# Seven block products for the last four gate tiles of a fused transformer layer

## The chip, the cores and the metric

The kernel runs on one core of a Trainium2 chip. The metric is the device time of one execution in microseconds (us). A core has five engines with queues of their own: TensorE (PE in the profile; its weight loads are PEld), VectorE (DVE), ScalarE (ACT), GpSimd (POOL) and SyncE (SP), which here only issues DMAs. They meet through semaphores. Operands lie in SBUF, matmul results in eight PSUM banks of 128x512 float32.

## The reference, cut to what matters

One layer, 1024 tokens, width 1024. The input is modulated, projected by one large matrix, and the last 2048 columns of that projection, after a sigmoid, gate the two attention branches:

```python
h = x * (1.0 + scale1) + shift1
proj = h @ w_in + b_in                       # q, k, v of both branches, then the gates
g_a, g_b = jnp.split(jax.nn.sigmoid(proj[..., OFF_GA:]), 2, axis=-1)
y = (g_a * (o_a @ w_branch_a) + g_b * (o_b @ w_branch_b)) @ w_out
```

The attention, the LayerNorms and a convolutional feed-forward part follow. The 2048 gate columns are 16 tiles of 128 columns. A gate tile is a 128x1024 block of the transposed weight times the 1024x1024 input `h`.

## The kernel before, in words

Each float32 factor is split into a high part rounded to the matmul type and the low rest (`split`, L335 to L342: a cast, then a subtraction). A product is three matmuls, high by high, high by low, low by high (`mm3`, L344 to L347), each 128x128 by 128x512.

The projection stage is a list `steps`, walked in one loop (L966). First come the q columns of branch B, then by `GORD` (L39) three gate tiles, the first half of q of branch A (group "qa"), four gate tiles, its second half ("qb": the change's title calls it the second q half), four gate tiles (7 to 10), group "ka" (keys and values of token tiles 0 to 4), gate tile 11, group "kb" (token tiles 5 to 7 and the two context tiles, called 8 and 9), and gate tiles 12 to 15. A gate tile is two steps, one for each half of the tokens (`gate`, L908): eight input tiles `hT[k]`, each a pair of high and low 128x1024 tiles, times the weight pieces, 24 matmuls a step. A step of kb is 15 matmuls.

Weights come by SP five steps ahead (`wload1`, three `raw` buffers) and are split three steps ahead (`wpair`, `wsplit`, four pairs of `wp` buffers): high part on ScalarE, low part on VectorE for q, k and v, on GpSimd for the gates.

Beside the steps runs a queue of side work. `side_step` (L932) takes one more entry from it and gives each entry in flight its next stage. `kv_post` (L628) is the side work of a key/value tile: stage 1 adds the bias out of PSUM and turns the first key (VectorE), copies the values (ScalarE, GpSimd) and takes the norm (its power on GpSimd, L555); stage 2 turns the second key and splits both into `ks`; stage 3 transposes `ks` on TensorE (`ktr`, L664). Two `kv` buffers serve the ten tiles, so a tile starts when the one two before it is through. `qprep` is that of the first two attention units. `mods` doles out 48 reductions (L445) that make the modulation vectors, from weights that SP loads (`mload`); the last falls into ka.

Through ka, VectorE and SP take the source order (`manual_schedule`, L959). After it all engines, and TensorE all along, take an order that a scheduler fixes when the kernel is built: it prefers what stands earlier in the source, among what it holds to be ready. On the chip each engine follows the fixed list.

Memory: 19 slots of 4 KB a partition (`ht`, `hput`). After ka all are taken: eight by the q tiles `Q0_t` and `Q1_t` of the two branches, ten by keys and values, one by the rotary table `ropet`. The attention stage follows with an order of its own for all engines; unit by unit it reads the q tiles, branch A first.

## Time and profile before

| | us |
|---|---|
| three runs | 1531.91, 1532.15, 1530.88 (median 1531.91) |
| profiled execution | 1530.37 |
| its span, first to last instruction | 1528.6 |
| TensorE busy in the span | 1512.9 |
| VectorE / ScalarE / GpSimd busy | 1144.8 / 802.1 / 773.5 |
| last gate matmul ends, attention starts | about 333.5 after the span's start |

In the rows of a timeline the columns are start, duration, engine, source line, operation, output, inputs, shapes and count; in brackets stands the idle time of the engine before the instruction and what ended it. In rows of groups they are line, engine, operation, output from inputs, shapes and count, then busy us and mean ns of one, then idle us and what ended it. A row of a stretch gives its length, then busy us and instruction count of each engine, the granted TensorE clock, the busy share of the DMA engines and GB/s. Matmuls overlap: the cost of one in a row is the distance of two starts, not the duration shown.

### The profile page before, as it was taken

The page shows a single profiled execution, that of the slowest core. Times are in us where ns is not written, and L with a number is a line of the kernel's source. Part 1 is how long each engine was busy: PE and PEld are TensorE (multiplying, and loading weights), DVE is VectorE, ACT ScalarE, POOL GpSimd, SP SyncE. Part 2 cuts the span into 40 slices and gives each one's busy share as a digit, 9 for nine tenths or more (in the row PEclk, how much of TensorE's full clock was granted, in tenths as well). Part 3 has the DMA queues.
Part 4 walks back from the last instruction along what each step waited for, and adds up shares of the span by engine and source line. Part 5 has one row for each costly group of instructions (what it writes and reads, how often), then busy time and mean ns, then how long its engine had stood idle before and what let it go on. Part 6 is the DMA issues. An engine that isn't in the chain of part 4 may idle for free. (4 is left out here: it accounts for less than half of the span.)

```text
span 1528.6 us, 21924 instructions
## 1 busy us (share of the span) xinstructions
PE 1512.9 (99%) x7652; PEld 1269.9 (83%) x7652; DVE 1144.8 (75%) x1719; ACT 802.1 (52%) x1404; POOL 773.5 (51%) x737
## 2 busy tenths in 40 slices
PE   9999999999999999999999999999999999999997
PEld 7888888888988888888788988888888888888886
DVE  7488847627776777787665878888888887656797
ACT  5422223449887777798332574444444444435543
POOL 0365303418887565574333556666676674021063
PEclk9999999999999999999999999999999999999999
DMA  9667663312256663742460222333334446996723
GB/s 379 236 234 254 213 239 110 100 49 56 57 151 157 176 149 79 169 95 68 169 173 35 97 86 108 112 110 112 112 102 111 110 111 177 373 281 207 253 91 111
DMA packets 111873, 229.73 MB, mean 150 GB/s; under 512 B 13489, under 2 KB 27313, under 8 KB 111666
## 3 DMA queue, kind: packets, MB, share of 16 engines
q1 hardware_dynamic: 96464, 199.20, 39.0%
q0 software_dynamic: 10400, 20.19, 8.4%
q10 hardware_dynamic: 4898, 8.94, 1.6%
q8 instruction: 60, 0.98, 0.3%
q14 instruction: 51, 0.42, 0.1%
HBM read 177.09 MB, written 65.87 MB: 159 GB/s over the span
## 5 line engine op out<-in xcount | busy, mean ns | idle before, releaser
L1151 DVE TENSOR_TENSOR lo<-pt,hi 128x512 fp32r<-128x512 f32 x188 | 126.4, 688 | 42.8 <-ACT hi L1145 41.3
L342 DVE TENSOR_TENSOR ld<-rd,hd 128x1024 fp32r<-128x1024 f32 x77 | 97.8, 1287 | 49.6 <-ACT hd L337 47.4
L1145 ACT CAST hi<-pt 128x512 fp32r<-128x512 f32 x188 | 109.6, 584 | 47.3 <-PE pt L808 39.1
L337 ACT CAST hd<-rd 128x1024 fp32r<-128x1024 f32 x77 | 79.4, 1050 | 85.8 <-PE p L347 55.7
L345 PE MATMUL p<-hd 128*128 128x512 f32 x264 | 103.2, 391 | 0.0
L346 PE MATMUL p<-ld,hd 128*128 128x512 f32 x264 | 102.8, 389 | 0.2 <-DVE ld L342 0.2
L347 PE MATMUL p<-hd,ld 128*128 128x512 f32 x264 | 102.8, 389 | 0.0
L817 PE MATMUL av<-lo,VT 128*128 128x512 f32 x236 | 101.5, 435 | 0.2 <-POOL lo L1151 0.2
L817 PE MATMUL av<-hi,VT 128*128 128x512 f32 x236 | 100.5, 433 | 0.0
L347 PE MATMUL g<-hh,wlg 128*128 128x512 f32 x256 | 99.7, 390 | 0.4 <-POOL wlg L342 0.4
L345 PE MATMUL g<-hh,whg 128*128 128x512 f32 x256 | 99.9, 390 | 0.0
L346 PE MATMUL g<-hl,whg 128*128 128x512 f32 x256 | 99.6, 389 | 0.0
L754 DVE TENSOR_SCALAR_CACHE_REDUCE p<-s,cvt,nmc 128x1024 f32<-128x1024 f32 x64 | 85.8, 1340 | 16.4 <-PE s L721 9.3
L342 POOL TENSOR_TENSOR wlg<-wg,whg 128x512 fp32r<-128x512 f32 x32 | 45.3, 1423 | 99.3 <-ACT whg L337 93.7
L763 ACT ACTIVATE p<-p,nm 128x1024 f32<-128x1024 f32 x64 | 74.0, 1157 | 13.0 <-DVE p L754 12.4
L808 PE MATMUL pt<-ident,p 128*128 128x128 f32 x512 | 76.8, 272 | 0.0
L808 PEld LDWEIGHTS pt<-ident,p 128*128 128x128 f32 x512 | 62.7, 140 | 15.4 <-DVE lo L1151 0.2
L337 ACT CAST wS<-s 128x512 fp32r<-128x512 f32 x76 | 45.3, 620 | 52.1 <-POOL s L1465 51.3
L720 PE MATMUL s<-KL,q 128*128 128x512 f32 (+2 forms) x184 | 72.4, 393 | 0.0
L721 PE MATMUL s<-KL,q 128*128 128x512 f32 (+2 forms) x184 | 69.0, 375 | 0.2 <-DMA q<-q 0.2
L337 ACT CAST wA<-ru 128x512 fp32r<-128x512 f32 x57 | 35.5, 623 | 59.6 <-PE d L347 31.8
L342 DVE TENSOR_TENSOR wS<-s,wS 128x512 fp32r<-128x512 f32 x57 | 55.5, 1000 | 11.1 <-ACT wS L337 11.1
(432 smaller groups left out, 5019.2 us busy)
## 6 DMA issues: line engine op xcount, KB each, us to landing
wml<-in_wmodT_dram SPq DMA_DIRECT2D x48, 512.0 KB
ru<-in_w_up_dram SPq DMA_DIRECT2D x38, 512.0 KB
rd<-td SPq DMA_DIRECT2D x55, 256.0 KB
rd<-sd SPq DMA_DIRECT2D x44, 256.0 KB
rd<-in_w_dn_dram SPq DMA_DIRECT2D x33, 256.0 KB
wm<-in_wmodT_dram SPq DMA_DIRECT2D x16, 512.0 KB
wg<-in_w_g_dram SPq DMA_DIRECT2D x32, 256.0 KB
sgd<-sg ACTq DMA_DIRECT2D x32, 256.0 KB
```

Source lines behind the costliest of these rows:

```text
L337: cast[:] = [nc.scalar.copy(hi, src).ins]
L342: low[:] = [lo_eng.tensor_tensor(out=lo, in0=src, in1=hi.bitcast(F32), op=ALU.subtract).ins]
L345: nc.tensor.matmul(ps, a[0], b[0], start=start, stop=False, skip_group_check=resumed)
L346: nc.tensor.matmul(ps, a[0], b[1], start=False, stop=False, skip_group_check=resumed)
L347: return nc.tensor.matmul(ps, a[1], b[0], start=False, stop=stop, skip_group_check=resumed).ins
L720: nc.tensor.matmul(o, self.q1[:, hs], ks, start=True, stop=False)
L754: nc.vector.tensor_scalar(out=p if self.br else p[:, self.pad + 1:SINK + 1], in0=self.sv[h], scalar1=self.scale()[:, hs] if self.br else - ...
L763: nc.scalar.activation(o, i, AF.Exp, bias=self.nm[:, hs], scale=-1.0, accum_out=acc)
L808: nc.tensor.transpose(tr[:, h * P:(h + 1) * P], src, ident)
L817: nc.tensor.matmul(self.av, v, self.parts[n][low], start=first, stop=self.left == 0)
L1145: nc.scalar.copy(hi, units[u].parts[n])
L1151: e.tensor_tensor(out=lo, in0=src, in1=hi.bitcast(F32), op=ALU.subtract)
```

## The change

Gate tile 11 moves from before kb to behind it, and tiles 12 to 15 are done otherwise. Two tiles are a pair. The pair's weights are a 2x2 matrix of blocks (tile by half of the 1024 inputs), `h` is a 2x2 matrix of blocks (half of the inputs by half of the tokens), and the eight block products of their product become seven, P1 to P7, of sums of blocks: fourteen `product` steps for two pairs, each four input tiles times three matmuls, 12 matmuls.

- **Input sums.** Sums need exact float32 inputs, so `x` is loaded again (`xload`, eight tiles of 512 KB), modulated (`xscale`, ScalarE) and summed in place (`xsums`, four subtractions of 128x512 for each pair of input tiles k and k+4, VectorE). They lie in the slots of the q tiles, which are first written to device memory (`away`, eight times 512 KB) and read back near the end (`qback`). Of the four groups of sums, group 0 and group 1 stand in gate tiles 9 and 10 (these, 7 to 10, follow the second q half), group 2 in ka, group 3 behind the first product. Summed inputs are split (`tsplit`) by ScalarE into the second halves of `hT[0..3]`, which gate tile 11 reads last, and into new tiles `TL[0..3]`: `TL[0]` takes the slot of `ropet`, `TL[k]` that of input tile k+3. The low parts of P6 are GpSimd's, the others VectorE's.
- **Weight sums.** P1, P2 and P4 use plain blocks and the old loads. The other blocks are loaded by `block_in`; `bsums` (GpSimd, four sums a pair) makes P5's, P6's, P7's and P3's weights of them. The first pair's blocks a11 and a22 go into the slot of input tile 7.
- **Outputs.** VectorE adds products out of PSUM (`vsum`, five a pair), then sigmoid and store as before.
- **Order.** From gate tile 11 to the end of the stage TensorE takes the source order.

The diff, cut to its core:

```diff
-GORD = 3, 4, 4, 1, 4
+GORD = 3, 4, 4, 0, 1
+    SRC = {"P1": (0, 0), "P2": (0, 1), "P4": (1, 1)}
+    SUM = {"P5": (0, 0), "P7": (1, 0), "P6": (1, 1), "P3": (0, 1)}
...
+    plain = len(steps)
+    steps += [("s", n, p) for n, p in (("P1", 0), ("P1", 1), ("P2", 0), ("P2", 1), ("P4", 0), ("P4", 1), ("P6", 0),
+                                       ("P5", 0), ("P6", 1), ("P5", 1), ("P7", 0), ("P7", 1), ("P3", 0), ("P3", 1))]
+    def away(br, t):
+        nc.sync.dma_start(qd[br, t], Q[br, t])
+    def xplace(k):
+        return ((1, 0), (1, 4), (0, 2), (0, 6), (1, 2), (1, 6), (0, 4), (0, 0))[k]
+    def xload(k):
+        X[k] = onto(hslot["Q%d_%d" % xplace(k)], [P, T], F32, f"xs{k}")
+        nc.sync.dma_start(X[k], xT[k])
+    def xsums(k):
+        a, b = k, k + 4
+        for o, p, q in ((xs(a, 1), xs(a, 1), xs(a, 0)), (xs(b, 1), xs(b, 1), xs(a, 1)),
+                        (xs(b, 0), xs(b, 0), xs(b, 1)), (xs(a, 0), xs(b, 1), xs(a, 0))):
+            nc.vector.tensor_tensor(out=o, in0=p, in1=q, op=ALU.subtract)
+    todo = {(7, 0): [(away, 1, 0), (away, 1, 2)], (7, 1): [(away, 1, 4), (away, 1, 6)],
+            (8, 0): [(xload, 0), (xload, 4)], (8, 1): [(xload, 1), (xload, 5)], (9, 0): [(xscale, 0)],
+            (9, 1): [(xscale, 1), (xsums, 0)], (10, 0): [(xsums, 1)], ("ka", 0): [(away, 0, 2)],
+            ("ka", 1): [(away, 0, 4)], ("ka", 2): [(xload, 2), (away, 0, 6)], ("ka", 3): [(xload, 6), (away, 0, 0)],
+            ("ka", 4): [(xload, 3)], ("ka", 5): [(xscale, 2)], ("ka", 6): [(xsums, 2)]}
+    TP = {"P4": (4, 0, 0), "P6": (4, 1, 1), "P5": (0, 1, 0), "P7": (0, 0, 1)}
+    def tsplit(n, k):
+        d, hf, m = TP[n]
+        hi = hT[k][m][:, HALF:T]
+        if k not in TL:
+            TL[k] = onto(hslot["Q%d_%d" % xplace(3 + k) if k else "ropet"], [P, T], R32, f"tl{k}")
+        split(xs(d + k, hf), hi, TL[k][:, hsl(m)], nc.scalar, nc.gpsimd if n == "P6" else nc.vector)
...
+        if n == plain - 2:
+            inorder.enter_context(tc.manual_schedule(engines={mybir.EngineType.PE}))
+        if gi == "s":
+            product(k, a)
+            m = n - plain
+            side_step()
+            if m == 0:
+                xsums(3)
+                for q in (3, 0, 1, 2):
+                    tsplit("P4", q)
+                    tsplit("P6", q)
+                block_in(0, 1, 0, bias_place("b21a"))
+                t = onto(hslot["Q0_0"], [P, 2, HALF], F32, "bA")
+                block_in(0, 0, 0, t[:, 0])
+                block_in(0, 1, 1, t[:, 1])
+            elif m == 1:
+                bsums(0, 0)
+            elif m == 3:
+                for b in ((1, 1, 0), (1, 0, 0), (1, 1, 1), (1, 0, 1), (0, 0, 1)):
+                    block_in(*b, pw("b%d%d%d" % b))
+            elif m == 4:
+                with tc.issue_after(last_sum[0]):
+                    bsums(1, 0)
+                    bsums(0, 1)
+                    bsums(1, 1)
+            elif m == 5:
+                for q in range(4):
+                    tsplit("P5", q)
+            elif m == 8:
+                qback((0, 0, 7))
+                for q in range(4):
+                    tsplit("P7", q)
+                qback((0, 2, 0), (0, 4, 1), (0, 6, 2), (1, 0, 3))
+            elif m == 11:
+                qback((1, 2, 4), (1, 4, 5), (1, 6, 6))
+            continue
         if gi == "g":
             gate(k, a)
+            early(k, a)
+            if n >= plain - 2:
+                if a == 0:
+                    xload(7)
+                else:
+                    xscale(3)
```

## The prediction

> **What bounds the kernel now.** I read the first lines of the page, then TensorE's timeline and ScalarE's sigmoids at the end of the projection stage.

> ```profile
> span 1528.6 us, 21924 instructions
> PE 1512.9 (99%) x7652; PEld 1269.9 (83%) x7652; DVE 1144.8 (75%) x1719; ACT 802.1 (52%) x1404; POOL 773.5 (51%) x737
> ```

> TensorE is busy for 99% of the span, so work taken from it counts in full unless a new wait fills the place.

> ```profile
> 247.35 0.39 PE L345 MATMUL g<-hh,whg 128*128 128x512 f32 x1
> ...
> 258.24 0.46 PE L664 MATMUL ktr<-identr,ks 128*128 128x128 f32 x4
> 258.53 0.46 PE L345 MATMUL acckb<-whkb,hh 128*128 128x512 f32 x1
> ...
> 287.83 0.39 PE L347 MATMUL acckb<-whkb,cl 128*128 128x512 f32 x1
> ```

> Gate tile 11 takes 258.24 - 247.35 = 10.89 us for 48 matmuls, 0.227 each: a row's 0.39 is not its cost. A group of four transposes costs 0.29. kb ends at 288.1.

> ```profile
> 328.24 0.69 ACT L920 ACTIVATE sg<-g,bgc 128x512 f32<-128x512 f32 x1 [4.75 <-PE g L347]
> 333.68 0.69 ACT L920 ACTIVATE sg<-g,bgc 128x512 f32<-128x512 f32 x1 [4.76 <-PE g L347]
> 334.39 1.28 ACT L1010 ACT_TABLE_LOAD   x1
> 336.40 1.23 POOL L1029 TENSOR_SCALAR pa<-negsink 128x1 f32<-128x1 f32 x8
> 336.62 0.73 ACT L763 ACTIVATE pa<-pa,nm 128x513 f32<-128x513 f32 x1 [0.73 <-POOL pa L1029]
> ```

> The last steps follow each other every 5.44 us, the time of their 24 matmuls, and ScalarE waits for TensorE each time: the end of the stage is TensorE's alone.

> **What goes.** Eight half tiles of 24 matmuls become fourteen products of 12: 192 become 168. The 24 that go are one such step: **-5.44 us**. Nothing else leaves or enters TensorE; gate tile 11 and the transposes only move.

> **What is added on the way there.** I looked at the stretches in which the q tiles leave and three groups of sums are made, and at an early one for the DMA rate.

> ```profile
> 20.00:40.00 20.00, 20.00 (x90) 16.57 (x89) 17.86 (x25) 12.39 (x12) 0.00 (x0) 1.00 1.03 405
> 177.00:200.00 23.00, 23.00 (x104) 19.03 (x103) 17.19 (x19) 5.27 (x9) 12.90 (x9) 1.00 0.61 213
> 220.00:247.40 27.40, 27.40 (x123) 22.69 (x122) 16.87 (x34) 6.18 (x10) 3.24 (x2) 1.00 0.57 183
> 207.22 0.69 DVE L342 TENSOR_TENSOR wlka<-wka,whka 128x512 fp32r<-128x512 f32 x1 [12.99 <-ACT whka L337]
> L478 ACT ACTIVATE xr<-xr,modc 128x1024 f32<-128x1024 f32 x7 | 8.7, 1245 | 0.2
> ```

> DMA: four stores and four loads of 0.52 MB in some 22 us add 190 GB/s to 213: 403, what the early stretch moved (405). In ka four stores, three loads and the kb loads that now come sooner, about 4.6 MB in 27.4 us, add 168 to 183: 351. It fits, if barely; at the lower rate that 183 GB/s at a share of 0.57 implies (321) ka's loads end 2.6 us late. SP stands in order with weight loads behind a store's wait, but each reload has two steps, 6.8 us or more, behind its store, and weights are split three steps ahead. Cost 0; without that cover up to 2.6.

> VectorE's groups 0 and 1 fall beside a wait of 12.99 us; I take each sum as a low part's subtraction, 0.6 (below). Group 2 and its scaling (two of 1.25) stand in ka, where VectorE has 10 us free and ScalarE 21; the low weights of kb queue behind them three steps early. Cost 0, or the group's 2.4 if that lead is used up.

> kb now follows ka at once, so its side work loses the cover of gate tile 11.

> ```profile
> 246.60:272.40 25.80, 25.80 (x130) 21.47 (x129) 24.87 (x97) 11.57 (x34) 11.11 (x14) 1.00 0.28 90
> 246.60 0.68 DVE L633 TENSOR_TENSOR kv<-accka,bias_kv 128x512 f32<-128x512 f32 x1
> 248.00 0.68 DVE L633 TENSOR_TENSOR kv<-accka,bias_kv 128x512 f32<-128x512 f32 x1
> ```

> kb wants five PSUM banks while ka still holds five of eight. Two are emptied by 248.7; the fourth is wanted at 247.4 + 9 x 0.227 = 249.4. Cost 0, or the 0.7 of one such add. VectorE is 24.87 of 25.80 busy while it serves ka's five tiles, packing 0.964; kb's end is 276.9 now (288.1 - 10.89 - 0.29), so this work still ends before.

> **The place that decides** is from there to P6. Its first VectorE work, tile 5 of kb, is complete at 285.54 - 11.18 = 274.4.

> ```profile
> 289.39 0.28 DVE L559 TENSOR_TENSOR kv<-kv,ssk 128x128 f32<-128x128 f32 x1
> 290.26 1.37 DVE L559 TENSOR_TENSOR kv<-kv,ssk 128x128 f32<-128x128 f32 x1
> 290.20 1.29 POOL L342 TENSOR_TENSOR wlg<-wg,whg 128x512 fp32r<-128x512 f32 x1
> 285.54 1.37 DVE L633 TENSOR_TENSOR kv<-acckb,bias_kv 128x512 f32<-128x512 f32 x2 [2.52 <-PE acckb L347]
> ```

> The same VectorE instruction takes 0.28 alone and 1.37 when GpSimd started 0.06 before it; it ends just behind GpSimd's. So most SBUF work of the two engines runs one after the other. [...]

> ```profile
> 258.50 0.68 DVE L342 TENSOR_TENSOR wlkb<-wkb,whkb 128x512 fp32r<-128x512 f32 x1
> 259.10 0.28 DVE L532 TENSOR_TENSOR ktp<-kv,ropet 128x128 f32<-128x128 f32 x1
> L559 DVE TENSOR_TENSOR kv<-kv,ssk 128x128 f32<-128x128 f32 x5 | 1.6, 322 | 0.4 <-POOL ssk L555 0.4
> L341 DVE CAST ks<-kv 128x256 fp32r<-128x256 f32 x5 | 1.4, 281 | 0.0
> L342 DVE TENSOR_TENSOR ks<-kv,ks 128x256 fp32r<-128x256 f32 x5 | 2.1, 411 | 0.0
> L540 DVE TENSOR_TENSOR kv<-ktp 128x128 f32<-128x128 f32 x6 | 1.7, 281 | 0.0
> L538 DVE TENSOR_TENSOR ktp<-kv,tbk 128x64 f32<-128x64 f32 x6 | 1.1, 212 | 0.0
> L532 DVE TENSOR_TENSOR ktp<-kv,tbk 128x128 f32<-128x128 f32 x3 | 0.8, 278 | 0.0
> L342 POOL TENSOR_TENSOR wlg<-wg,whg 128x512 fp32r<-128x512 f32 x6 | 7.8, 1296 | 4.9 <-ACT whg L337 4.9
> L645 POOL TENSOR_TENSOR VT<-kv,VT 128x256 fp32r<-128x256 f32 x5 | 3.9, 781 | 4.1 <-ACT VT L637 4.0
> L655 POOL TENSOR_TENSOR kv<-kv,gcol 128x128 f32<-128x128 f32 x2 | 0.9, 460 | 0.6 <-PE g L347 0.4 <-DVE kv L559 0.2
> ```

> VectorE, kb's five tiles: 1.6 + 1.4 + 2.1, two turns of three tiles 1.7 + 12 x 0.212 + 6 x 0.278, in all 11.0 for 39 instructions; successive ones overlap by 0.08 (0.68 against a distance of 0.60), so 7.9. With the last group of sums (4 x 0.6), P4's low parts (4 x 0.6) and P6's first low weight (0.6): 13.3. GpSimd: five weight splits 6.5 (P1 to P4 but the first), 3.9, 0.9, P6's low parts 4 x 1.3, two weight sums 2 x 1.3 (two inputs of that size, as in the split): 19.1. Together **32.4 us**.

> TensorE in source order, from 276.9: gate tile 11 10.9, five transposes 1.5, P1 and P2 10.9: the transposes of tile 9 are due at 300.2; with them and two P4 (0.3 + 5.4) P6 is due at 305.9. From 274.4 that is 31.5. Packed without a gap the sums are 0.9 late, at packing 0.964 (33.6) 2.1. Bounds: 0, if part of it overlaps, and 9.2 (below). I take the middle of the packed two, **+1.5**, since that row is the nearest.

> Behind the stalled P6 are only products. P5's and P7's splits have one product and their own first chunks (2.7 + 2) as cover for four casts and four subtractions of 0.6, which chase each other; the rest of the weight sums has 10 us of GpSimd. The 4 MB read back go while DMA is at 0.11.

> ```profile
> 307.40:333.50 26.10, 26.10 (x122) 21.64 (x121) 0.00 (x0) 4.88 (x8) 2.59 (x2) 1.00 0.11 41
> PE pt L808 <- ACT pa L763: 0.7, 2, 0.4
> ```

> VectorE's zero there is room for the ten output adds. At the hand-over the last sigmoid stands behind one more add, 0.7. Attention's first exponential waits for GpSimd at 336.62, 0.7 after the table load and its small exponential; so **+0.1**, or 0.7 at most. The two waits of TensorE (0.7) stay.

> **Sum:** -5.44 + 1.5 + 0.1 = -3.8: 1530.37 becomes 1526.5 for the profiled execution (1.8 of it outside the span). The median shown is 1.54 higher, 1531.91, so the forecast is **1528.1**. A run of this kernel can't tell less than 0.2%, 3.1 us, from no change: the bounds are 1528.8 and 1535.0.

> **The rivals.**

> *No wait at all* (0.13). The engines overlap more than I count: -5.3, **1526.6**. For it: VectorE's adds from PSUM, and GpSimd's powers (L555) beside which VectorE rows aren't long. Against: the stretch at 0.964.

> *The reload is late* (0.30). P4's and P6's splits form a ring: `TL[3]` needs the slot of input tile 6, which `q=2` reads last, and so on, while a11 and a22 need the slot of input tile 7, which `q=3` reads. If all but P6's weight is done first, 29.2 / 0.964 = 30.3, it starts at 304.7.

> ```profile
> 242.97 0.90 SPq L873 DMA_DIRECT2D cx<-in_ctxT_dram  x2
> 245.53 0.60 ACT L877 ACTIVATE cx<-cx,modx 128x256 f32<-128x256 f32 x1 [0.98 <-DMA cx<-in_ctxT_dram]
> ```

> A load takes 2.6; then two sums 2.6 and the split 1.3: ready at 311.2, 5.3 late. -5.44 + 5.3 + 0.1: **1531.9**, the same. For it: this order in the source. Against: tiles 8 and 9 can fill the load's gap.

> *Source order holds TensorE at tile 9* (0.25), the case on the other side. Before, the scheduler put these transposes where it liked; now P4 stands behind them. Tile 9's second stage stands behind the tile sums and the weight sums in the source. If VectorE and GpSimd take these first, its `ks` comes after 32.4 + 1.3 (third sum) = 33.7, 35.0 packed: 309.4 against 300.2, 9.2 late. -5.44 + 9.2 + 0.1 = +3.9: **1535.8**. It decides slower from a wait of 8.4 on, `ks` behind 308.6. [...] Against: before, tile 9 was through in 22 us.

> That the change does not do what it says would be a hand-over that isn't TensorE's; the sigmoid rows exclude more than the 0.7 above.

> **How the numbers follow.** The forecast case, a wait of 0.5 to 2.4, has 0.32; with no wait 0.13 that makes faster 0.45, same 0.30, slower 0.25. The forecast, likeliest by little and beside the no-wait case in sign, alone has 1527.1 to 1529.0. The range goes from 1526.2 (no wait, a little spread) to 1537.0 (the slower rival and the 0.7 of the hand-over).

> **What would show it.** 24 matmuls fewer; 168 under the product tiles at 0.227. In the list of waits, TensorE before P6's first matmul, for VectorE's low weight: 1 to 2 us; 5 us there speaks for the reload; a wait of the `ktr` transposes for VectorE `ks` of 9 us for the source order. The stretch from 274 to 306 with VectorE and GpSimd nearly full. What would make me wrong elsewhere: TensorE waiting in ka or kb for low weights (DMA too slow, or VectorE behind group 2), or at P7, or in the first attention units for a q tile read back late.

## The result, and the profile after

The changed kernel takes 1546.47 us (median of 4 runs, 1545.1 to 1547.27) against 1531.43 of the kernel before beside it: ratio 1.0097, 95% interval 1.008 to 1.0115. It is 15 us slower, where 3.8 us faster was forecast. The profiled execution took 1545.1 us, 1.8 of it outside the span. Each profile read below shows one execution; those of e11 and e19 are the slowest of their kernels' runs, that of e17 the fastest.

The first lines of the page, changed kernel:

```profile
span 1543.3 us, 22040 instructions
PE 1516.0 (98%) x7628; PEld 1268.2 (82%) x7628; DVE 1186.3 (77%) x1765; ACT 824.7 (53%) x1436; POOL 792.2 (51%) x747
```

TensorE has 24 instructions fewer (7628 for 7652) and is yet busy for 3.1 us more: some of its matmuls became slower. The span is 14.7 longer, so the rest of the loss is idle time. Where it lies, the stretches between TensorE's stage borders show. In each row: length, busy us and count of each engine, granted TensorE clock, DMA share, GB/s. First the kernel before, kb and then gate tiles 12 to 15:

```profile
258.53:288.06 29.53, 29.53 (x147) 24.56 (x146) 20.24 (x64) 14.18 (x44) 12.55 (x14) 1.00 0.39 119
288.06:333.48 45.42, 45.42 (x213) 37.69 (x212) 16.15 (x50) 12.60 (x32) 13.73 (x16) 1.00 0.16 57
```

The changed kernel, in order: kb; gate tile 11 and P1 of both pairs; P2 of both (behind a wait of 2.2 us, which no row shows); P4 of both with the wait before P6; P6 of the first pair; P5 of the first; the other six products:

```profile
246.47:282.06 35.59, 32.23 (x145) 25.35 (x144) 34.33 (x112) 15.88 (x44) 13.47 (x15) 0.95 0.36 111
282.06:299.91 17.85, 17.85 (x89) 14.71 (x87) 16.29 (x49) 8.01 (x22) 9.66 (x12) 1.00 0.14 46
302.12:308.40 6.28, 6.28 (x33) 5.18 (x33) 4.35 (x7) 4.91 (x15) 4.26 (x5) 1.00 0.57 173
308.40:318.21 9.81, 6.21 (x26) 4.24 (x26) 1.75 (x2) 0.62 (x1) 8.21 (x7) 0.99 0.33 107
318.21:323.90 5.69, 5.65 (x12) 4.01 (x13) 3.74 (x3) 3.32 (x7) 5.53 (x5) 0.50 0.14 49
323.90:330.58 6.68, 4.61 (x13) 2.83 (x12) 6.62 (x8) 2.29 (x6) 3.41 (x3) 0.76 0.21 78
330.58:347.74 17.16, 17.16 (x73) 13.94 (x72) 10.51 (x15) 7.59 (x12) 0.93 (x2) 0.97 0.67 222
```

kb: 35.59 against 29.53, **+6.1**, VectorE busy 34.33 of it. Between the second and third row TensorE stands still: **+2.2** before P2. The fourth row should be two products, 2 x 2.72: **+4.4**. P6: 5.69 for 2.72 at a clock of 0.50, **+3.0**. P5: **+4.0**. Six products in 17.16 for 16.32: **+0.8**. In all +20.5; less the 5.44 saved, and less 0.9 because ka ends at 246.47 and not 247.35, that is 14.2: the stage ends at 347.74 and not 333.48. The last 0.4 of the span lies behind the stage.

TensorE's waits in the changed kernel, those of 1 us or more that the kernel before has not (us in all, times, longest):

```profile
PE ktr L670 <- DVE ks L343: 2.3, 1, 2.3
PE ly L346 <- ACT whP L338: 2.2, 1, 2.2
PE lz L347 <- DVE tl L343: 2.1, 2, 1.3
PE lx L346 <- ACT u L1080: 2.0, 1, 2.0
PE lw L348 <- POOL wlgP L343: 1.4, 1, 1.4
PE sx L727 <- DMA q<-q: 1.0, 1, 1.0
```

The first five lie in this stage, in kb, P6, P5, P2 and P4, and each ends with another instruction, on three engines; no single culprit stands there. (`lx`, `lw`, `ly`, `lz` are the banks of P1 and P2, P4, P6 and P7, P5 and P3; `u` is P1's copy, `tl` the low inputs `TL`, `whP` and `wlP` the split of a summed weight, `wlgP` the low part of a plain one, `b`, `b21a` and `bA` the loaded blocks, `bA` a11 and a22; L338 is the cast of a split, L343 its subtraction, L670 the transposes, L866 `block_in`, L1051 `bsums`.) The last, 1.0 us, is a new wait in attention, at 479 us, far behind its first units. The timelines of three places tell how the waits arise.

**kb.** TensorE waits 2.25 us with a transpose, and kb's matmuls stand behind it. VectorE and GpSimd at that time:

```profile
270.39 0.29 DVE L565 TENSOR_TENSOR kv<-kv,ssk 128x128 f32<-128x128 f32 x1 [0.18 <-POOL ssk L561]
270.60 1.48 DVE L343 TENSOR_TENSOR ks<-kv,ks 128x256 fp32r<-128x256 f32 x1
```
```profile
270.45 1.35 POOL L343 TENSOR_TENSOR wlg<-wg,whg 128x512 fp32r<-128x512 f32 x1
272.14 0.37 PE L670 MATMUL ktr<-identr,ks 128*128 128x128 f32 x2 [2.25 <-DVE ks L343]
```

The `ks` subtraction, 0.41 alone, takes 1.48: GpSimd's split began 0.15 before it, and it ends 0.28 behind that split (272.08, 271.80). The prediction saw the same in the trace before (1.37 for 0.28) and counted on it one stage later. It makes 1.1 of the 2.25 us; the rest is that VectorE came to this tile late: its cast began at 269.92, when TensorE was waiting already.

**P6.** GpSimd, then SP, ScalarE and VectorE of the changed kernel:

```profile
310.45 1.75 POOL L343 TENSOR_TENSOR tl<-xs,hl 128x512 fp32r<-128x512 f32 x1
312.15 1.29 POOL L343 TENSOR_TENSOR wlgP<-wP,whgP 128x512 fp32r<-128x512 f32 x1
314.88 1.29 POOL L1051 TENSOR_TENSOR b21a<-bA,b21a 128x512 f32<-128x512 f32 x1 [1.44 <-DMA bA<-in_w_g_dram]
316.25 1.26 POOL L1051 TENSOR_TENSOR bA<-bA,b21a 128x512 f32<-128x512 f32 x1
318.82 6.44 POOL L1051 TENSOR_TENSOR b<-b,b 128x512 f32<-128x512 f32 x4
312.22 0.80 SPq L866 DMA_DIRECT2D bA<-in_w_g_dram  x2
317.54 0.62 ACT L338 CAST whP<-bA 128x512 fp32r<-128x512 f32 x1 [10.51 <-POOL bA L1051]
318.19 2.90 DVE L343 TENSOR_TENSOR wlP<-bA,whP 128x512 fp32r<-128x512 f32 x2 [7.16 <-ACT whP L338]
324.06 4.05 DVE L343 TENSOR_TENSOR tl<-xs,hh 128x512 fp32r<-128x512 f32 x3
```

That is the rival "the reload is late", step by step: the last reader of input tile 7's slot ends at 312.20, SP issues the reload at 312.22, GpSimd gets it at 314.88, two sums, ScalarE's cast at 317.54, P6 at 318.21. VectorE's low part of that weight then takes 2.90 for two and P5's low parts 4.05 for three, beside GpSimd's four sums of 1.61: 1.4 each for 0.6.

**The clock.** TensorE's timeline in kb, from the third matmul behind the wait on:

```profile
273.38 0.39 PE L348 MATMUL acckb<-whkb,hl 128*128 128x512 f32 x1
273.61 0.59 PE L346 MATMUL acckb<-whkb,hh 128*128 128x512 f32 x1
273.99 0.63 PE L347 MATMUL acckb<-wlkb,hh 128*128 128x512 f32 x1
274.42 0.63 PE L348 MATMUL acckb<-whkb,hl 128*128 128x512 f32 x1
...
276.98 0.43 PE L348 MATMUL acckb<-whkb,ch 128*128 128x512 f32 x1
277.25 0.39 PE L346 MATMUL acckb<-whkb,ch 128*128 128x512 f32 x1
```

From 273.61 to 277.0 the starts are 0.43 apart and not 0.23: half clock for 3.4 us, 1.5 us behind the end of a wait of 2.25. These matmuls take 1.6 us more than at full clock. The stretch doesn't, however: e4 below has kb with the same work at a clock of 1.00, and its kb takes 36.38 us, VectorE busy for 35.16 of them; it is VectorE that sets its length.

### The profile page after: what moved, and what is told of

Read it like the earlier page. It is cut to its first block, busy times and chain, and to the rows that moved or that the text cites. A ratio compares the mean times of both kernels' runs of the same rounds, so it can differ in the third digit from the quotient of the medians.

```text
span 1543.3 us, 22040 instructions
## 1 busy us (share of the span) xinstructions
PE 1516.0 (98%) x7628; PEld 1268.2 (82%) x7628; DVE 1186.3 (77%) x1765; ACT 824.7 (53%) x1436; POOL 792.2 (51%) x747
## 4 chain that ended last, share of the span: by engine, by line
PE 86%; DVE 6%; DMA 2%; POOL 2%; issue 2%; ACT 1%; SPq 0%; DVEq 0%; ACTq 0%; POOLq 0%
PE av L823 7%; PE pt L814 6%; PE s L726 3%; PE s L727 3%; PE g L348 3%; PE g L347 3%; PE g L346 3%; PE p L348 2%; PE p L346 2%; PE p L347 2%; PE c L346 2%; PE d L346 2%; PE a L348 2%; PE a L346 2%; PE c L348 2%; PE d L348 2%
## 5 line engine op out<-in xcount | busy, mean ns | idle before, releaser
L343 DVE TENSOR_TENSOR ld<-rd,hd 128x1024 fp32r<-128x1024 f32 x77 | 96.6, 1271 | 51.1 <-ACT hd L338 47.5
L338 ACT CAST hd<-rd 128x1024 fp32r<-128x1024 f32 x77 | 79.5, 1050 | 87.8 <-PE p L348 61.4
L347 PE MATMUL p<-ld,hd 128*128 128x512 f32 x264 | 103.2, 391 | 0.4 <-DVE ld L343 0.4
L348 PE MATMUL g<-hh,wlg 128*128 128x512 f32 x192 | 74.9, 390 | 0.4 <-POOL wlg L343 0.4
L346 PE MATMUL g<-hh,whg 128*128 128x512 f32 x192 | 75.0, 391 | 0.0
L347 PE MATMUL g<-hl,whg 128*128 128x512 f32 x192 | 74.8, 390 | 0.0
L338 ACT CAST wS<-s 128x512 fp32r<-128x512 f32 x76 | 45.2, 620 | 51.7 <-POOL s L1656 50.9
L338 ACT CAST wA<-ru 128x512 fp32r<-128x512 f32 x57 | 35.5, 623 | 61.7 <-PE d L348 33.2
L1345 POOL TENSOR_TENSOR lo<-ptr,hi 128x512 fp32r<-128x512 f32 x48 | 62.5, 1301 | 2.0
L343 DVE TENSOR_TENSOR wS<-s,wS 128x512 fp32r<-128x512 f32 x57 | 56.8, 1024 | 4.9 <-ACT wS L338 4.9
```

What stands on the lines that cost most here:

```text
L338: cast[:] = [nc.scalar.copy(hi, src).ins]
L343: low[:] = [lo_eng.tensor_tensor(out=lo, in0=src, in1=hi.bitcast(F32), op=ALU.subtract).ins]
L346: nc.tensor.matmul(ps, a[0], b[0], start=start, stop=False, skip_group_check=resumed)
L347: nc.tensor.matmul(ps, a[0], b[1], start=False, stop=False, skip_group_check=resumed)
L348: return nc.tensor.matmul(ps, a[1], b[0], start=False, stop=stop, skip_group_check=resumed).ins
L1345: e.tensor_tensor(out=lo, in0=src, in1=hi.bitcast(F32), op=ALU.subtract)
```

## The experiments

The theory after the trace: **the seven products are too close to their inputs.** The chain of splits and sums on VectorE, GpSimd and ScalarE is longer than the matmul work that covers it, each consumer in TensorE's fixed list waits in turn, and each wait may cost a stretch of half clock. The rivals: TensorE's source order; the one late reload; kb's lost neighbour; the sums in ka. The time holds more than the stage: from the stage's end to the span's end the traces of these kernels have 1194.0 us (e8) to 1198.5 (e14), though no edit is aimed there. So where a difference is of 2 us or less, the stage's end in the trace stands beside the time.

| kernel | us | ratio to before, 95% |
|---|---|---|
| e1: only gate tile 11 moved | 1532.97 | 1.0009 (0.9999 to 1.0019) |
| e2: without the source order | 1546.26 | 1.0098 (1.0083 to 1.0113) |
| e3: reload into other buffers | 1545.74 | 1.0098 (1.0081 to 1.0114) |
| e4: weight sums on VectorE | 1541.53 | 1.0065 (1.005 to 1.008) |
| e6: third group of sums later | 1543.66 | 1.0086 (1.0069 to 1.0103) |
| e7: filler before P6 | 1546.18 | 1.0097 (1.0082 to 1.0112) |
| e8: gate tile 10 behind kb too | 1537.87 | 1.0043 (1.0028 to 1.0058) |
| e9: e8 and weight sums on VectorE | 1533.85 | 1.002 (1.001 to 1.003) |
| e10: a gate tile between ka and kb | 1539.3 | 1.0055 (1.0041 to 1.0068) |
| e11: gate tiles between and behind | 1531.79 | 1.0003 (0.9994 to 1.0013) |
| e12: e11, second P6 before first P5 | 1531.89 | 1.0006 (0.9997 to 1.0015) |
| e13: e12, ka's transposes later | 1531.95 | 0.9999 (0.999 to 1.0008) |
| e14: the change, ka's transposes later | 1549.19 | 1.0109 (1.0096 to 1.0123) |
| e15: e13, kb's work first | 1535.22 | 1.0019 (1.001 to 1.0028) |
| e16: e12, kb's work first | 1535.68 | 1.0027 (1.0016 to 1.0037) |
| e17: e15, kb's transposes later too | 1533.49 | 1.0013 (1.0004 to 1.0022) |
| e18: e17, source order from P1 on | 1533.54 | 1.0012 (1.0003 to 1.0021) |
| e19: e17, P1 copied by VectorE | 1533.38 | 1.0008 (0.9999 to 1.0017) |

**e1, gate tile 11 alone** (in the kernel before):

```diff
-GORD = 3, 4, 4, 1, 4
+GORD = 3, 4, 4, 0, 5
```

> The kernel before with one thing of the change: gate tile 11 goes behind group kb instead of between ka and kb (GORD 3, 4, 4, 0, 5); no products, no early stores, loads or sums. Theory A, kb's 6.5 us of waits and slow clock in the changed kernel come from the missing gate tile (VectorE has to finish ka's five tiles and kb's splits in kb's own 29 us): kb takes 33 to 36 us here too and the time is 1534 to 1538. Theory B, they come from the third group of input sums and its loads, which this kernel lacks: kb takes under 31 us and the time stays within 1 us of 1531.4.

kb takes 30.74 us, 1.2 more than before, and the interval of the ratio reaches down to no change. Neither theory in full: the missing gate tile is about 1.2 of kb's 6.1 us.

```profile
247.68:278.42 30.74, 29.84 (x146) 24.25 (x144) 30.04 (x102) 13.91 (x41) 15.67 (x17) 1.00 0.36 108
```

VectorE is busy 30.04 of 30.74: it has no room left here for the sums.

**e6, the third group of sums later** (in the changed kernel):

```diff
-            ("ka", 4): [(xload, 3)], ("ka", 5): [(xscale, 2)], ("ka", 6): [(xsums, 2)]}
+            ("ka", 4): [(xload, 3)], ("ka", 5): [(xscale, 2)]}
...
+                xsums(2)
                 xsums(3)
```

> The changed kernel with its third group of input sums (four subtractions on VectorE) issued behind kb with the fourth, and not at ka's seventh step. Theory A, that group stands ahead of kb's own work on VectorE, which is full there (18.7 of 20 us): without it kb takes 31 to 33 us instead of 35.6, and behind kb the 2.4 us come back in part: 1542 to 1545. Theory B, kb is late for another reason (the loads, or kb's splits by themselves): kb stays above 35 us and the time rises by up to 2 us.

```profile
246.85:279.29 32.44, 29.94 (x146) 24.35 (x144) 31.59 (x109) 15.40 (x43) 13.74 (x15) 1.00 0.42 130
```

Theory A: kb loses 3.1 us less. So kb's 6.1 are 1.2 (e1), 3.1 of the sums, and some 1.7 not taken apart; with the sums in ka, kb takes 35.6 to 36.6 in five traces (the changed kernel, e2, e3, e4, e7), so these sizes are good to about 1 us. The time falls by 2.8.

**e2, without TensorE's source order**: the line that enters it at `plain - 2` is taken out.

> The changed kernel without TensorE's source order behind kb: the scheduler places its instructions from gate tile 11 on. Theory A, TensorE waits for data that come late whatever its order: the time stays at 1544 to 1548. Theory B, the source order is what makes TensorE stand idle while other products could run: the waits before P2, P4 and P6 (6 us in all) shrink and the time is 1541 or less.

The time stays, and so do the waits. Row by row TensorE's list up to the end of the stage is the same in both traces: left alone, the scheduler chooses the source order too. So forcing it cost nothing; whether another order would wait less this run can't tell.

**e3, the reload elsewhere**:

```diff
-                t = onto(hslot["Q0_0"], [P, 2, HALF], F32, "bA")
-                block_in(0, 0, 0, t[:, 0])
-                block_in(0, 1, 1, t[:, 1])
+                block_in(0, 0, 0, raw("a11"))
+                block_in(0, 1, 1, raw("a22"))
```

> The changed kernel with the blocks a11 and a22 of the first pair loaded into two buffers of the ring of raw weights, which are free once P2's and P4's weights are split (about 306 and 309 us), and no longer into the slot of input tile 7 (free at 312.2). Theory A, P6 of the first pair waits for this reload and the clock falls behind that wait: P6 starts 1.5 to 3 us earlier, its 12 matmuls take about 3 us instead of 5.7, and the time falls by 3 to 5 us, to 1541 to 1543. Theory B, GpSimd and ScalarE are the bound of that chain (the weight sums and splits of P2 to P6 in one line): P6 starts less than 1 us earlier and the time falls by less than 1.5 us.

P6 waits no more, and the time is less by 0.7 only. P4 of both pairs with what follows, P6, P5:

```profile
308.18:318.06 9.88, 7.45 (x27) 5.63 (x26) 4.27 (x4) 1.88 (x4) 9.72 (x7) 0.83 0.42 135
318.06:321.40 3.34, 2.94 (x13) 2.07 (x11) 1.50 (x2) 1.61 (x4) 3.26 (x4) 1.00 0.24 83
321.40:329.01 7.61, 5.13 (x13) 3.02 (x13) 7.61 (x8) 2.58 (x6) 4.89 (x4) 0.78 0.00 0
```

P6 starts at 318.06, as before at 318.21. GpSimd is busy 9.72 of the 9.88 us ahead of it: it did a weight sum first, P4's low weight came later (a wait of 2.4 for 1.4), and the slow clock moved to P4. The reload was what ended the last wait, but without it GpSimd's work alone lasts as long. Theory B. In this trace the stage ends at 345.67, 2.1 earlier, and the part behind it is 1.9 longer: the reload may hold up to 2 us of the loss, not the 3 to 5 of theory A.

**e4, the weight sums on VectorE**:

```diff
-            last_sum[:] = [nc.gpsimd.tensor_tensor(out=o, in0=a, in1=b, op=op).ins]
+            last_sum[:] = [nc.vector.tensor_tensor(out=o, in0=a, in1=b, op=op).ins]
```

> The changed kernel with the eight weight sums on VectorE instead of GpSimd. Theory A, VectorE's low parts for P5 (4.05 us for one row in the profile) are blocked by GpSimd's sums beside them, 1.6 us each: with the sums on VectorE at 0.6 us each P5's two products lose under 2 us instead of 4 and P6's weight is ready about 1.3 us earlier: 1541 to 1543. Theory B, VectorE itself is full there and only gets more work: the time stays at 1545 or goes up.

Theory A: 5 us less (1541.53 for 1546.47). P6 and P5 of the first pair:

```profile
318.02:323.28 5.26, 4.70 (x13) 3.43 (x13) 5.23 (x10) 4.89 (x10) 0.00 (x0) 0.68 0.15 53
323.28:326.63 3.35, 3.29 (x14) 2.10 (x12) 3.35 (x7) 0.63 (x2) 0.77 (x2) 1.00 0.45 157
```

With GpSimd at zero, VectorE does the same low parts and the sums besides, and P5 takes 3.35 for 6.68. Three of P5's low parts take 1.89 us for 4.05: of P5's loss these low parts' longer time beside GpSimd's sums was nearly all. P6's weight is no earlier, which theory A had wrong.

**e7, filler before P6**:

```diff
+        if (n, p) == ("P6", 0):
+            for j in range(12):
+                nc.tensor.matmul(ps, filler[0:P, 0:P], late_b("P2", j % 4)[0], start=True, stop=True)
```

> The changed kernel with 12 idle matmuls (result overwritten) on TensorE right before P6 of the first pair, where it waits 2.3 us: 2.7 us of work that serves only to keep the array busy. Theory A, P6 runs at half clock (0.427 us a matmul) because of the wait before it: with the filler its matmuls take 0.227 and the clock row of that stretch is 1.00; P6 ends 2 us earlier, but P5 then waits longer for the low parts, so the time falls by 0 to 2 us. Theory B, the half clock follows from something else (all the load on the chip, the operands): P6 stays at 0.427 and the time rises by 0.4 to 1 us.

The filler, then P6:

```profile
316.68:319.43 2.75, 2.75 (x13) 2.25 (x12) 0.42 (x1) 0.62 (x1) 2.59 (x3) 1.00 0.30 107
319.43:322.73 3.30, 3.06 (x13) 1.99 (x11) 2.38 (x2) 1.68 (x3) 3.22 (x3) 1.00 0.21 79
```

P6 runs at full clock, 3.30 us for 5.69. Without the wait of 2.16 there is no half clock here. The time is the same: P5 began at 324.31 (323.90 in the changed kernel), then waited for its casts and low parts and had the slow clock itself (0.64 from 324.31 to 331.98). P6 at full clock won nothing here, since P5's inputs came no earlier.

**e10, a gate tile between ka and kb again**: `GORD = 3, 4, 3, 1, 1`.

> The changed kernel with one gate tile (the eleventh) between ka and kb again, one before fewer (GORD 3, 4, 3, 1, 1); all else as it is, the third group of sums in ka too. Theory A, kb stands too near to ka: VectorE is behind with ka's five tiles and the sums, so kb's matmuls and transposes wait; with 10.9 us more between them kb takes under 31 us instead of 35.6, nothing is lost behind it that was not lost before, and the time falls by 3 to 6 us, to 1540 to 1543. Theory B, the backlog lasts through the gate tile too, or comes from the loads: kb stays above 34 us and the time at 1545 or more.

1539.3, 7 us less than the changed kernel, more than was expected. kb is 32.77, not under 31, but what stood behind it was done earlier too: the waits before P2 and in P4 are gone, those of P6 (2.0) and P5 (2.6) stay.

**e8 and e9, gate tile 10 behind kb**:

```diff
-GORD = 3, 4, 4, 0, 1
+GORD = 3, 4, 3, 0, 2
...
-            (9, 1): [(xscale, 1), (xsums, 0)], (10, 0): [(xsums, 1)], ("ka", 0): [(away, 0, 2)],
+            (9, 1): [(xscale, 1), (xsums, 0)], (10, 0): [(xload, 7), (xsums, 1)],
+            (10, 1): [(xscale, 3), (xsums, 2)], (11, 0): [(xsums, 3)], ("ka", 0): [(away, 0, 2)],
```

> The changed kernel with gate tile 10 moved behind kb as well (GORD 3, 4, 3, 0, 2), input tiles 3 and 7 loaded and scaled there one gate earlier, and the second to fourth group of sums issued behind kb, beside gate tiles 10 and 11. Theory A, VectorE, GpSimd and ScalarE have one serial chain up to P6 for which the change leaves too little matmul time: with 10.9 us more of it the waits before P2, P4 and P6 (6 us, and the slow clock behind them) go and kb loses under 2.5 us; P5 alone still waits: 1528 to 1533. Theory B, the chain starts from the end of the gate tiles whatever stands before them (the split into the upper half can't begin earlier): P4, P6 and P5 wait as now and the time is 1538 or more.

> As the kernel with gate tile 10 behind kb, and also the eight weight sums on VectorE instead of GpSimd. Theory A (chain too long for its cover): 1 to 4 us less than without, 1526 to 1530, P5's loss under 1 us. Theory B (start of the chain fixed by the gates' end): 4 us less than without, as in the pair measured before, but still 1534 or more.

e8: the waits before P2, P4 and P6 go, as theory A has it, but P5 waits 4.4 us and kb takes 36.75, 7.2 more than before, so 1537.87, just under theory B's bound and 5 us above theory A's. e9: P6 and all behind it run, P5 takes 4.14; 1533.85. The 4.0 us won are those of theory B and the time is just under its 1534; but P4 and P6 wait no more, as theory A has it. What is left is P5's 1.4 and 7 us in kb.

**e11 and e12, gate tiles between and behind**: `GORD = 3, 4, 2, 1, 2`, weight sums on VectorE, the scales in gate tiles 9 to 11 and

```diff
+            (10, 0): [(xload, 7), (xscale, 2), (xsums, 0)], (10, 1): [(xscale, 3), (xsums, 1)],
+            (11, 0): [(xsums, 2)], (11, 1): [(xsums, 3)]}
```

and in e12 also

```diff
-("P6", 0), ("P5", 0), ("P6", 1), ("P5", 1)
+("P6", 0), ("P6", 1), ("P5", 0), ("P5", 1)
```

> The version that the runs so far point to: gate tile 9 between ka and kb, gate tiles 10 and 11 behind kb (GORD 3, 4, 2, 1, 2), the scales in gate tiles 9 to 11, all four groups of input sums in gate tiles 10 and 11, the weight sums on VectorE. Theory A (each loss is a lack of cover for a chain of VectorE, ScalarE and GpSimd): kb loses under 2 us (7 in the kernel with both gate tiles behind and none between), the products under 3, so 1526 to 1530, below the kernel before. Theory B (four groups of sums behind kb and kb's own five tiles are too much for VectorE in 22 us of gate tiles): P4 or P6 waits again by 3 us or more, 1531 to 1535.

> As the version with gate tiles between and behind, with the second pair's P6 ahead of the first pair's P5, and its three weight sums one step earlier. Theory A, P5 of the first pair starts before its low parts are there (0.8 us of wait and the slow clock behind it): one product more as cover takes its loss from 1.4 to under 0.4 us, and the time is 0.5 to 1.5 us less than without. Theory B, the second pair's weight sums then come late: P6 of the second pair waits 1 us or more and the time is the same or more.

e12's group kb, gate tiles 10 and 11, all fourteen products:

```profile
237.78:271.24 33.46, 31.35 (x146) 25.71 (x146) 24.06 (x73) 15.28 (x45) 10.82 (x12) 0.95 0.41 122
271.24:294.81 23.57, 23.57 (x118) 19.60 (x116) 17.87 (x52) 11.71 (x32) 14.25 (x17) 1.00 0.32 108
294.81:333.21 38.40, 38.40 (x170) 31.58 (x170) 24.66 (x35) 18.89 (x33) 9.34 (x8) 1.00 0.51 169
```

The products now run without a gap, 14 in 38.40, 2.74 each, as theory A wants. e12's first row still holds a wait of 2.1 us for a `ks` and the slow clock behind it, and the time equals the kernel before: kb takes 33.46, 3.9 us more than before, and the stage ends at 333.21 for 333.48. So most of what the products save is lost in kb. On the time both forecasts (1526 to 1530; 0.5 to 1.5 less in e12) were missed.

**e13 and e14, ka's transposes one step later** (`e14` in the changed kernel, `e13` in e12):

```diff
-        return [s1] + [lambda: None] * GAP + [s2, s3]
+        return [s1] + [lambda: None] * GAP + [s2] + [lambda: None] * (t < 5) + [s3]
```

> As the version with the second pair's P6 first, but with the transposes of ka's five tiles one step (3.6 us of kb) later in the source. Theory A, kb's 4.4 us there (a wait of 2.1 for VectorE's split, then the slow clock) come from a transpose that stands in TensorE's list before its data are there: kb loses under 2 us and the time is 2 to 3.5 us less than without, 1528 to 1530. Theory B, VectorE is simply late and the next instruction waits in the transpose's place (kb's accumulators leave their banks later): kb's loss stays above 3.5 us and the time within 1 us.

> The changed kernel with the transposes of ka's five tiles one step later in the source, nothing else. Theory A (their place in TensorE's list): kb takes 31 to 33 us instead of 35.6 and the time falls by 2 to 4 us. Theory B (VectorE is behind with ka's tiles and the third group of sums, whatever TensorE's list): kb stays above 34.5 us and the time within 1.5 us of the changed kernel.

e14's kb is 3 us shorter, 32.58, as A has it, and the time is 2.7 us *longer*: P2 now waits 5.0 us for ScalarE's copy of P1. In e13 the wait for `ks` is gone and one of 2.3 for a context split (`ch`) stands in its place. e13 is theory B's, in kb (34.29 us) and in the time: the next wait took the place of the one removed. e14 is neither's: theory A has kb right and the time wrong, theory B both wrong. In its trace the stage ends at 348.46, only 0.7 later; the rest of its loss lies behind the stage.

**e15 to e18, kb's own work first.** In e13's lists ScalarE's scale of input tile 7 and VectorE's sums stand ahead of kb's last context splits. e15 (from e13) and e16 (from e12) queue them behind:

```diff
+            with ExitStack() as behind:
+                if k >= 10:
+                    for i in last_c:
+                        behind.enter_context(tc.issue_after(i))
+                early(k, a)
```

> As the version with the transposes one step later, but the scales and sums of gate tiles 10 and 11 are queued behind kb's last context split on ScalarE and VectorE. Theory A (kb's loss there is work taken ahead of kb's own): the wait of 2.3 us for a context split goes, kb loses under 2 us instead of 4.6, the products still lose under 1 us, and the time is 1528 to 1530, below the kernel before. Theory B (VectorE is late anyway, or the sums come late for P4): kb or P4 and P6 lose 3 us or more and the time stays within 1 us of the kernel before.

> The same, with the transposes of ka's tiles where the changed kernel has them. Theory A (a transpose early in TensorE's list costs its own wait): kb loses 3 to 4.5 us, a wait of about 2 for VectorE's split of a k tile and the slow clock behind it; 1530 to 1532. Theory B (that wait too came from the sums and scales taken first): kb loses under 2 us and the time is within 0.5 us of the other kernel.

Against its own matmuls and transposes kb loses 0.6 and 0.9 us now, and the loss comes up in gate tile 11, where neither theory of e15 had it; e16, within 0.5 us of e15, is theory B's. e15's kb, then gate tiles 10 and 11 up to P1, 28.79 for 23.57 in e12:

```profile
238.28:268.11 29.83, 29.83 (x149) 24.82 (x148) 22.45 (x71) 16.76 (x43) 7.83 (x9) 1.00 0.45 124
268.11:296.90 28.79, 25.32 (x117) 20.84 (x116) 25.03 (x65) 12.85 (x37) 19.04 (x20) 0.94 0.32 101
288.73 0.53 PE L670 MATMUL ktr<-identr,ks 128*128 128x128 f32 x4 [3.46 <-DVE ks L343]
```

There gate matmuls stand behind a transpose of kb in TensorE's list. Whether the scheduler's own order would have them there too, no run of this version shows. e17 puts kb's transposes one step later too (`* (t < 5)` goes), e18 besides begins the source order with the first product.

> As the version with kb's work first, with the transposes of kb's five tiles one step later as well. Theory A (a transpose too early in an in-order list costs a wait and the slow clock behind it, 6 us; VectorE has room over the whole of kb and the gate tiles): kb, gate tiles 10 and 11 and the products lose under 3 us together and the time is 1527 to 1530. Theory B (VectorE, GpSimd and ScalarE are short of time for the whole): the 5 to 6 us come up at the next consumer, the products, and the time stays at 1531 to 1536.

> As that, and TensorE's source order begins with the first product, not in gate tile 11. Theory A: within 1 us of the kernel with all transposes later (1527 to 1530), since nothing waits in the gate tile there. Theory B: 1531 or more here too.

kb and the gate tiles lose little (under 1 us in kb); P2 waits 3.1 and 3.0 us for ScalarE's copy of P1. Theory B in both, by 1533.5. Row by row TensorE's list in e18 is that of e17, so e18 tells nothing of the order: it is e17 once more.

**e19, P1's copy on VectorE** (`nc.vector.tensor_copy` in `product`).

> As the kernel with all ten transposes one step later, but P1's result is copied out of its bank by VectorE (idle there 1.7 and 2.4 us at a time) and not by ScalarE. Theory A (each loss is one late instruction with TensorE's list behind it): P2 starts at once, 2.5 to 3.3 us earlier, nothing else loses more than 1 us, and the time is 1529.5 to 1531, below the kernel before by under 0.15%. Theory B (ScalarE and VectorE are short of time there): the next consumer, P4 or P6, waits instead and the time stays at 1532 or more.

P2 waits 3.5 us in two pieces, now for VectorE. Theory B by the time, though the wait stayed at P2 and didn't go to P4 or P6: so it was not ScalarE alone that made the copy late. None of these versions is measurably faster than the kernel before.

## Why the prediction was wrong, point by point

- **-5.44 for the 24 matmuls**: right. 7628 instructions for 7652, and the fourteen undisturbed products of e12 take 2.72 to 2.83 each.
- **The way there, cost 0**: right for the DMAs (ka ends at 246.47, no later than before), wrong for the third group of sums. I gave "the group's 2.4 if that lead is used up" as the other end; e6 measures 3.1.
- **"kb directly behind ka, cost 0" failed first**: +6.1. I compared when VectorE's work on ka's tiles ends with when kb ends. But kb has consumers inside: transposes and context splits stand in TensorE's list with kb's matmuls behind them. With VectorE at 34.33 of 35.59 each of these is late. The deciding sum began with tile 5 of kb complete at 274.4; VectorE took it up at 280.49. e1, e6 and e10 show the parts: the neighbour, the sums, the backlog passed on.
- **The wait before P6, +1.5**: it is 2.2, and 2.0 before P2 and 1.4 in P4 ahead of it, since the chain began later (kb's end 282.06, not 276.9) and its earlier consumers were not priced. That 2.2 lies near 1.5 is luck: the wait was forecast for VectorE's low weight, and it ended with ScalarE's cast behind the reload. My sum of 32.4 us had VectorE and GpSimd serial, all of it; no run shows that. In the trace before, VectorE's `kv` took 1.37 for 0.28 beside a GpSimd split, and beside GpSimd's copies of values a row of L538 0.57 for 0.21 and a cast of `ks` 0.84 for 0.28. But two adds out of PSUM kept their 0.69 beside a split (1.37 for both, at 285.54), a reduction its 0.27 beside a copy (287.56), and rows of 0.21 and 0.28 stayed so beside GpSimd's powers (288.48 to 290.23). ScalarE, whose casts, copies and sigmoids stand between the two, was left out.
- **The rival "the reload is late"** describes P6's wait exactly (ready at 317.5 to 318.2; 311.2 was worked out), but as price it was too small, and it isn't what the loss hangs on: e3 took it away and the time fell by 0.7.
- **"P5's splits have cover, cost 0" failed**: +4.0. I priced their subtractions at 0.6 although GpSimd had four weight sums at the same time; at 1.4 the cover is too short. e4 removes most of it. I had this longer time in the sum before P6 and forgot it behind.
- **Source order**: no cost in the changed kernel (e2 has the same order without being told; tile 9's transposes at 308.1 without a wait).
- **The clock was never priced**: matmuls at half clock took some 6 us more (kb 1.6, P6 about 2.4, P5 and the next product about 1.9). That isn't 6 us of the 20. e7 ran P6 at full clock and won nothing, and kb is no shorter where it has no half clock (e4: 36.38 for 35.59): behind operands that were late anyway it was hidden there. How much of the 20 it makes stays open.
- **Hand-over +0.1**: right. Attention's first exponential comes 3.22 us behind the last product (350.96 less 347.74), 3.14 before.

Why none of e11 to e19 is faster is argued here, not shown: TensorE was 99% busy before because VectorE, ScalarE and GpSimd had room beside the matmul work around kb. The change takes 5.44 us of that work and adds to all three (41.5, 22.6 and 18.7 us busy more over the span). Wherever one late instruction was moved out of the way (e14, e15, e17, e19), another took its place. What exactly limits that last line, an engine's total or the scheduler's fixed order in ScalarE's and VectorE's lists, stays open: VectorE is busy 13 to 18 of every 20 us from 240 to 320 in e17 and e19, so not full on average.

## What to carry to other kernels

Matmuls taken from a TensorE that hides three other engines are only won if these engines have room at every consumer, not in the sum over a stage: list each consumer in TensorE's order with the time at which its operand is ready. Look in the trace for VectorE subtractions of two SBUF tiles beside GpSimd work, and price them by what they took there: here 1.48 for 0.41 beside a split of 1.35, 1.4 for 0.6 beside sums of 1.61. And look for half clock behind TensorE's waits: in the changed kernel it came behind waits of 2.25, of 2.16 and of 1.34 and 0.73 in a row, for 3.41, 6.83 and 3.41 us, and not behind one of 2.05. In e7, where P6's matmuls ran at full clock, the time stayed, because the next product's operands came no earlier.

## What the hardware showed that I had not expected

What went ahead of half clock shows when the changed kernel is cut at these borders: how long TensorE idles within one window of 3.41 us, all waits in it together. Four windows, in the columns of a stretch: the first is the one with most of kb's wait, the second follows it; the last two share the wait before P2.

```profile
270.23:273.64 3.41, 1.50 (x12) 1.38 (x13) 3.25 (x9) 0.81 (x5) 1.71 (x3) 1.00 0.19 71
273.64:277.06 3.42, 3.42 (x10) 2.68 (x9) 2.96 (x11) 1.03 (x5) 2.45 (x4) 0.50 0.19 29
297.54:300.95 3.41, 2.54 (x14) 1.95 (x12) 2.83 (x3) 2.87 (x10) 3.19 (x5) 1.00 0.25 30
300.95:304.36 3.41, 2.24 (x10) 1.86 (x11) 2.40 (x5) 3.41 (x11) 2.85 (x3) 1.00 0.64 187
```

In the first TensorE idles 1.91 us (3.41 less 1.50) and the next window has half clock; in the last two it idles 0.87 and 1.17, and the clock stays. Between 235 and 350 us this trace has 29 whole windows at full clock: in three TensorE idles 1.76, 1.91 and 1.97 us, and half clock follows each; in the other 26 it idles 1.44 or less, and none is followed by it. Between 60 and 1400 us the same three stand against 384 windows with 1.67 or less. So in this trace the two kinds part between 1.67 and 1.76. Why the second stretch lasted 6.83 us and the others 3.41, it doesn't show.

So waits of one length can end either way. e17 and e18 have the same list for TensorE and nearly the same wait before P2, 3.06 and 2.98 us; in e17 the clock stays at 1.00 from 240 to 340, in e18 the matmuls behind the wait start 0.43 apart up to 306.8, with a clock of 0.83 from 300 to 320, and the stage ends 2.0 later. My estimate for e18, from these starts and a length of 6.83, is that half clock began at about 300.2, with some 2.1 us of the wait in the window before. How e17's wait lies in the windows was not shown.
